# Differential attention in 1024-key score tiles: a two-layer encoder trunk on one core

## The chip, the core and the metric

The kernel runs on one NeuronCore of a Trainium2 chip. TensorE (PE; its weight loads are listed apart as PEld) multiplies matrices into PSUM, VectorE (DVE) and ScalarE (ACT) read PSUM and SBUF, GpSimd (POOL) works on SBUF alone, and SyncE (SP) issues the transfers. Each engine takes its instructions in the order in which they stand and waits at semaphores for the others. The metric is the device time of one execution in microseconds. For each kernel several executions are timed; one more is recorded by the profiler.

## The reference, cut to what matters

Two layers run over 2048 tokens of width 1024. Layer 0 (two kinds of banded attention) and the projections of layer 1 stay as they are. What changes is layer 1's differential attention: eight heads, each with two score maps whose softmaxes are subtracted before the product with the values, for rows of 128 queries over all keys up to the end of their own 64-token chunk.

```
s1 = q1 @ k1.T * scale;  s2 = q2 @ k2.T * scale        # 128 queries x all keys so far
p1 = softmax(where(mask, s1, NEG_INF));  p2 = softmax(where(mask, s2, NEG_INF))
o  = (p1 - lam * p2) @ v
o  = rms_norm(o, subln_g) * (1.0 - lambda_init)
y  = (o * silu(gate)) @ w_out;  x = x + y
```

Row t (0 to 15) sees 128(t+1) keys, so a head has 128 x 136 = 17,408 key columns in each of its two maps.

## The kernel before, in words

Every float32 operand of a product is split into a high and a low part (names ending in H and L), and a product is made of two or three matmuls. Layer 1 first projects (names that begin with p1) and then mixes: this is `_mix1`, whose tiles have names that begin with c.

`scores(h, b, K, res)` treats a block of four rows of head h. For each row and each of the two maps (m) it cuts the keys into pieces of at most 512. A piece gets a PSUM tile of one bank (tag S, four buffers), two matmuls (L842, L843), a VectorE maximum with the sign turned (L846), from the second piece on a running minimum with the piece before (L848), and on ScalarE the exponential with that maximum as its bias and with its sum collected (L850, which shows as ACTIVATE and as a READ_ACCUMULATOR). The last piece's masked corner is overwritten first (L845). So pieces of one row have different biases. A row with several pieces gets factors e from the biases (L855), and a VectorE instruction weighs and adds the sums (L856); GpSimd copies the first map's sum into a column (L858). VectorE then makes the reciprocal (L862), the factor of the last piece (L863) and those of the others (L865). The two maps are put together piece by piece: GpSimd scales the first map's earlier pieces by e (L869) and the second map's by its factor (L874), and adds (L875); every fifth piece is scaled and added by VectorE in one instruction instead (L872, `COMB`). Pieces of the first map live in a pool of 28 tiles of 512 columns (`pp`, tag P0), those of the second in six (tag P1).

`values(h, b, V, res)` takes the finished rows of a block: per 128 keys it transposes the pieces of four rows on TensorE into one bank (L889), splits the result with ScalarE (L892) and VectorE (L893), and adds three matmuls of up to 512 columns into a PSUM tile (L897 to L899). The output goes through ScalarE (L904) to memory.

A third stream, `gates()`, makes the gate projection with dense matmuls (L198 to L200, tile cG). `pace` interleaves the three as they are written down: scores run ahead of values by at most `LAG1` units (a unit is 256 score columns or one transposed 128 x 128 piece), gates by their share. From this program order a scheduler sets the order on each engine; gate matmuls may not stand ahead of the score matmul noted in `self.anchor`. At the end of `pace`, and in the `weave` after it, come the norm and the gate product (`finish`, with two P1 tiles per head, L1006 and L1008) and the output projection (`out_tile`, whose PSUM tiles have the tag S and whose residual tiles have the tag P1). The pool `pp` also holds the weights of layer 1's projection, and at the end output weights.

Of the kernel before, what the change touches and what calls it, by code (L numbers as in the profile page):

```python
# [18 lines left out]
P = 128  # L19
S = 2048  # L20
# [48 lines left out]
class Trunk:  # L69
# [4 lines left out]
    COMB = 5  # L74
    LAST = (0, 3, 2, 1)
    BANKS1, LAG1, SHARE1 = (4, 2, 1, 1), 65, 1.0
# [131 lines left out]
    def _project(self, es, layer):  # L208
# [21 lines left out]
        def weight_tiles():  # L230

            i = chunks[0] % 12 if layer == 0 else None
            chunks[0] += 1
            for part in "HL":
                if layer == 1:
                    yield self.pp.tile([P, 512], F32R, tag="P0", name=n + "w" + part)
# [547 lines left out]
    def layer1(self, steps=("project", "mix")):  # L784
        pool = self.tc.tile_pool
        with pool(name="hv", bufs=2) as self.hv, pool(name="pp", bufs=28, side="right") as self.pp:
            if "project" in steps:
                self.project(1)
            if "mix" in steps:
                self.mix1()  # L790
# [5 lines left out]
    def _mix1(self, es):  # L796
# [19 lines left out]
        count = [0]  # L816

        def scores(h, b, K, res):
# [3 lines left out]
            for m in range(2):  # L822
                r = slice(m * HD, (m + 1) * HD)
                for part, q in (("qH", qd), ("qL", ql)):
                    nc.sync.dma_start(f32(q[0:HD, m, :]), s[part][h, r, tok])
                    nc.sync.dma_start(f32(q[HD:P, m, :]), s[part][h, r, tok])
            us = res["u"] = []
            l1 = small("l1", NTB)
            for j in range(NTB):
                t = b * NTB + j  # L830
                nk = (t + 1) * P
                cuts = [(c, min(nk, c + 512)) for c in range(0, nk, 512)]
                nb = len(cuts)
                js = slice(j * P, (j + 1) * P)
                pr = []
                for m in range(2):
                    nm, la, chunks = small("nm", 4), small("la", 4), []
                    for z, (c, ce) in enumerate(cuts):
                        wd = ce - c
                        ps = pS.tile([P, 512], F32, tag="S", name=n + "S")[:, :wd]  # L840
                        kt = K[z][m]
                        mm(ps, qd[:, m, js], kt[:, :wd], start=True, stop=False)  # L842
                        self.anchor = mm(ps, ql[:, m, js], kt[:, :wd], start=False, stop=True).ins  # L843
# [3 lines left out]
                        if z:  # L847
                            nc.vector.tensor_tensor(nm[:, z:z + 1], nm[:, z:z + 1], nm[:, z - 1:z], ALU.min)  # L848
                        chunks.append((sb if m else pp).tile([P, 512], F32, tag=f"P{m}", name=n + f"P{m}", bufs=6 if m else 28))
                        nc.scalar.activation(chunks[z][:, :wd], ps, AF.Exp, bias=nm[:, z:z + 1], accum_out=la[:, z:z + 1])  # L850
                        yield wd / 256
                    l, e = la[:, 0:1], None
                    if nb > 1:
                        e, l, pe = small("e", 4), small("l"), small("pe", 4)
# [264 lines left out]
```

## Time and profile before

| | us |
|---|---|
| three timed executions | 2973.82, 2973.92, 2978.35 (median 2973.92) |
| profiled execution, its own time | 2979.35 |
| its span, first to last instruction | 2977.6 |
| first and last score matmul of layer 1 (L843) begin | 1827.0 and 2698.8 |
| mean granted TensorE clock | 0.966 |

Rows of a profile name the line of the kernel, the engine, the operation, the tile written and the tiles read with their buffer numbers left out, the shapes (partitions x elements), the count, the busy time and the mean of one. In the views that have it, idle time of the engine just ahead of the instruction follows, and behind an arrow whoever released it. Rows of the windows give the start and end of a stretch, its length, and busy time per engine. Matmuls overlap: one's listed duration is longer than the distance to the next one's start.

### The profile page before, as it was taken

The numbers are of one execution on the slowest core, as the hardware profiler recorded it, in microseconds if no ns is written. First come the engines' busy times: TensorE is split into PE (matmuls) and PEld (weight loads), VectorE is DVE, ScalarE is ACT, GpSimd is POOL, SyncE is SP. The second block draws the span as 40 slices with busy tenths as digits, with TensorE's granted clock in tenths as the row PEclk, the third lists the DMA queues.
The fourth block names the chain that finished last, engine by engine and source line by source line (L and its number), as shares of the span: only waits on it lengthen the run. The fifth ranks groups of instructions, "written<-read, shape, count | busy, mean of one in ns | idle before, by whom it ended". The sixth has DMA issues, their size and how long they took to land. (4 is left out here: it accounts for less than half of the span.)

```text
span 2977.6 us, 45362 instructions
## 1 busy us (share of the span) xinstructions
PE 2738.9 (92%) x13672; PEld 2253.3 (76%) x13672; DVE 2113.1 (71%) x5516; ACT 1615.0 (54%) x4167; POOL 1537.2 (52%) x1774
## 2 busy tenths in 40 slices
PE   7999999997888889899999999899999999986898
PEld 5888888876777778777788887677777777864776
DVE  7652475156767775589638844999998999986673
ACT  4443543266656665343343323677776777765552
POOL 3542252145334343357645732776766777775552
PEclk9999999999999999999999999999999999997999
DMA  4673344569988885657884456356546546425443
GB/s 156 224 249 121 103 149 128 186 190 258 256 218 219 221 216 146 213 207 239 268 290 155 129 182 200 111 141 188 166 121 187 161 133 194 141 80 153 138 131 104
DMA packets 349973, 526.28 MB, mean 177 GB/s; under 512 B 42272, under 2 KB 143648, under 8 KB 349728
## 3 DMA queue, kind: packets, MB, share of 16 engines
q1 hardware_dynamic: 349728, 523.38, 59.7%
q8 instruction: 109, 1.79, 0.3%
q14 instruction: 136, 1.11, 0.1%
HBM read 354.42 MB, written 168.82 MB: 176 GB/s over the span
## 5 line engine op out<-in xcount | busy, mean ns | idle before, releaser
L850 ACT ACTIVATE cP<-cS,cnm 128x512 f32<-128x512 f32 (+3 forms) x640 | 399.4, 628 | 191.3 <-DVE cnm L848 111.9
L846 DVE TENSOR_REDUCE cnm<-cS 128x1 f32<-128x512 f32 (+3 forms) x640 | 374.7, 598 | 26.3 <-PE cS L843 21.8
L198 PE MATMUL p1mm<-p1wH,p1hH 128*128 128x512 f32 x768 | 304.7, 397 | 0.0
L199 PE MATMUL p1mm<-p1wL,p1hH 128*128 128x512 f32 x768 | 304.4, 396 | 0.0
L200 PE MATMUL p1mm<-p1wH,p1hL 128*128 128x512 f32 x768 | 302.9, 395 | 0.0
L842 PE MATMUL cS<-ck,cqd 128*128 128x512 f32 (+3 forms) x640 | 265.7, 417 | 36.7 <-ACT cP L850 29.2
L286 POOL TENSOR_TENSOR p0wL<-p0ws,p0wH 128x512 fp32r<-128x512 f32 (+1 forms) x128 | 155.5, 1248 | 276.7 <-ACT p0wH L285 263.7
L875 POOL TENSOR_TENSOR cP<-cP,cP 128x512 f32<-128x512 f32 (+3 forms) x256 | 284.5, 1126 | 3.3
L874 POOL TENSOR_SCALAR cP<-cP,ccs 128x512 f32<-128x512 f32 (+3 forms) x256 | 176.4, 698 | 170.3 <-DVE ccs L863 67.2
L198 PE MATMUL p0mm<-p0wH,p0hH 128*128 128x512 f32 (+1 forms) x640 | 237.6, 374 | 3.9 <-ACT p0vt L436 3.1
L843 PE MATMUL cS<-ck,cql 128*128 128x512 f32 (+3 forms) x640 | 237.5, 373 | 1.8 <-DMA cql<-qL 1.8
L199 PE MATMUL p0mm<-p0wL,p0hH 128*128 128x512 f32 (+1 forms) x640 | 237.7, 372 | 0.0
L200 PE MATMUL p0mm<-p0wH,p0hL 128*128 128x512 f32 (+1 forms) x640 | 237.5, 372 | 0.2 <-DVE p0hL L311 0.2
L286 POOL TENSOR_TENSOR p1wL<-p1ws,p1wH 128x512 fp32r<-128x512 f32 x128 | 167.8, 1333 | 95.3 <-ACT p1wH L285 80.7
L893 DVE TENSOR_TENSOR cptL<-ctr,cptH 128x512 fp32r<-128x512 f32 (+1 forms) x320 | 190.3, 597 | 17.9 <-ACT cptH L892 17.1
L842 PEld LDWEIGHTS cS<-ck,cqd 128*128 128x128 f32 x640 | 124.2, 194 | 82.9 <-ACT cP L850 67.6
L892 ACT ACTIVATE cptH<-ctr 128x512 fp32r<-128x512 f32 (+1 forms) x320 | 168.5, 535 | 33.2 <-PE ctr L889 32.6
L889 PE MATMUL ctr<-ident,cP 128*128 128x128 f32 x1088 | 181.5, 282 | 1.1 <-POOL cP L875 0.9
L198 PEld LDWEIGHTS p1mm<-p1wH,p1hH 128*128 128x128 f32 x768 | 145.1, 189 | 30.4
L200 PEld LDWEIGHTS p1mm<-p1wH,p1hL 128*128 128x128 f32 x768 | 145.0, 189 | 30.3 <-issue 0.2
L199 PEld LDWEIGHTS p1mm<-p1wL,p1hH 128*128 128x128 f32 x768 | 145.0, 189 | 29.2
L889 PEld LDWEIGHTS ctr<-ident,cP 128*128 128x128 f32 x1088 | 139.1, 145 | 36.0 <-issue 4.0
(311 smaller groups left out, 8011.1 us busy)
## 6 DMA issues: line engine op xcount, KB each, us to landing
p1ws<-in_od_w_in_dram SPq DMA_DIRECT2D x56, 512.0 KB, 4.4
p0ws<-in_ev_w_in_dram SPq DMA_DIRECT2D x48, 512.0 KB, 4.4
cqd<-qH SPq DMA_DIRECT2D x128, 128.0 KB, 4.4
cql<-qL SPq DMA_DIRECT2D x128, 128.0 KB, 4.3
cwH<-wgH SPq DMA_DIRECT2D x32, 512.0 KB, 4.6
cwL<-wgL SPq DMA_DIRECT2D x32, 512.0 KB, 5.8
mvB<-bv SPq DMA_DIRECT2D x24, 512.0 KB, 6.9
mvA<-av SPq DMA_DIRECT2D x24, 480.0 KB, 5.4
```

Source lines behind the costliest of these rows:

```text
L198: mm(ps, aH, bH, start=first, stop=False)
L199: mm(ps, aH, bL, start=False, stop=False)
L200: mm(ps, aL, bH, start=False, stop=last)
L286: nc.gpsimd.tensor_tensor(l[:, :width], ws[:, k, :width], f32(h[:, :width]), ALU.subtract)
L842: mm(ps, qd[:, m, js], kt[:, :wd], start=True, stop=False)
L843: self.anchor = mm(ps, ql[:, m, js], kt[:, :wd], start=False, stop=True).ins
L846: nc.vector.tensor_reduce(nm[:, z:z + 1], ps, AX.X, ALU.max, negate=True)
L850: nc.scalar.activation(chunks[z][:, :wd], ps, AF.Exp, bias=nm[:, z:z + 1], accum_out=la[:, z:z + 1])
L874: nc.gpsimd.tensor_scalar(p2, p2, cc, 1.0, ALU.mult, ALU.mult)
L875: nc.gpsimd.tensor_tensor(p1, p1, p2, ALU.add)
L889: nc.tensor.transpose(tp[:, (j - j0) * P:(j - j0 + 1) * P], us[j][kt // 4][:, kk:kk + P], self.ident)
L893: nc.vector.tensor_tensor(L[:, :wd], tp[:, :wd], f32(H[:, :wd]), ALU.subtract)
```

## The change

Score tiles take up to 1024 keys: tag S has two buffers of two banks each, where it had four of one bank (`BANKS1`). A tile gets two or four matmuls, one maximum and one exponential. A row has at most two pieces, so that the running minimum, the factor e and the sums occur once per map, in rows 8 to 15 alone. The weighted sum of the two collected sums, the last piece's factor and the other piece's factor are now one-column instructions on GpSimd (new L881, L886, L888); the copy of the sum is gone. The second map is always scaled on GpSimd (new L891); the earlier piece, 1024 wide, is scaled and added to it by VectorE (new L893), the last piece is added on GpSimd (new L895). `COMB` is gone.

Rows 0 to 3 and 4 to 7 stay groups of four; rows 8 to 15 are values groups of two rows, whose transposes put two times 128 keys of two rows in one bank and whose matmuls have 256 columns. Queries are still loaded per block of four (`queries`). The pool `pp` is cut into 8 tiles of 1024 (PA) and 12 of 512 (PB), P1 into 3 of 1024; the uses of the pool outside the attention follow. `LAG1` goes from 65 to 48.

```diff
-    COMB = 5
+    WIDE, NARROW = 8, 12
-    BANKS1, LAG1, SHARE1 = (4, 2, 1, 1), 65, 1.0
+    BANKS1, LAG1, SHARE1 = (2, 2, 1, 1), 48, 1.0
...
+        groups = [(4 * b + i, 4 * b + i + n) for b in range(NB) for n in ((4,) if b < 2 else (2,)) for i in range(0, 4, n)]
...
-                cuts = [(c, min(nk, c + 512)) for c in range(0, nk, 512)]
+                cuts = [(c, min(nk, c + 1024)) for c in range(0, nk, 1024)]
...
-                        ps = pS.tile([P, 512], F32, tag="S", name=n + "S")[:, :wd]
-                        kt = K[z][m]
-                        mm(ps, qd[:, m, js], kt[:, :wd], start=True, stop=False)
-                        self.anchor = mm(ps, ql[:, m, js], kt[:, :wd], start=False, stop=True).ins
+                        ps = pS.tile([P, 1024], F32, tag="S", name=n + "S")[:, :wd]
+                        for k in range(c, ce, 512):
+                            w = min(ce - k, 512)
+                            kt, o = K[k // 512][m], ps[:, k - c:k - c + w]
+                            mm(o, qd[:, m, js], kt[:, :w], start=True, stop=False)
+                            self.anchor = mm(o, ql[:, m, js], kt[:, :w], start=False, stop=True).ins
+                            if k + w < ce:
+                                yield w / 256
...
-                            nc.vector.tensor_tensor(nm[:, z:z + 1], nm[:, z:z + 1], nm[:, z - 1:z], ALU.min)
+                            nc.vector.tensor_scalar(nm[:, 1:2], nm[:, 1:2], nm[:, 0:1], None, ALU.min)
...
-                        nc.vector.tensor_tensor_reduce(pe[:, :nb], e[:, :nb], la[:, :nb], 1.0, 0.0, ALU.mult, ALU.add, l)
-                    if m == 0:
-                        nc.gpsimd.tensor_scalar(l1[:, j:j + 1], l, 1.0, 1.0, ALU.mult, ALU.mult)
+                        nc.gpsimd.tensor_scalar(l, la[:, 0:1], e, la[:, 1:2], ALU.mult, ALU.add)
...
-                nc.vector.scalar_tensor_tensor(cs[:, nb - 1:nb], la1, self.nlam, rl, ALU.mult, ALU.mult)
+                nc.gpsimd.tensor_scalar(cs[:, nb - 1:nb], rl, la1, self.nlam, ALU.mult, ALU.mult)
                 if nb > 1:
-                    nc.vector.tensor_scalar(cs[:, :nb - 1], e2[:, :nb - 1], cs[:, nb - 1:nb], None, ALU.mult)
+                    nc.gpsimd.tensor_scalar(cs[:, 0:1], e2, cs[:, 1:2], 1.0, ALU.mult, ALU.mult)
                 for z, (c, ce) in enumerate(cuts):
+                    nc.gpsimd.tensor_scalar(p2, p2, cs[:, z:z + 1], 1.0, ALU.mult, ALU.mult)
                     if z < nb - 1:
-                        nc.gpsimd.tensor_scalar(p1, p1, e1[:, z:z + 1], 1.0, ALU.mult, ALU.mult)
-                    count[0] += 1
-                    if count[0] % self.COMB == 0:
-                        nc.vector.scalar_tensor_tensor(p1, p2, cc, p1, ALU.mult, ALU.add)
+                        nc.vector.scalar_tensor_tensor(p1, p1, e1, p2, ALU.mult, ALU.add)
                     else:
-                        nc.gpsimd.tensor_scalar(p2, p2, cc, 1.0, ALU.mult, ALU.mult)
                         nc.gpsimd.tensor_tensor(p1, p1, p2, ALU.add)
...
+            each = NTB // (r1 - r0)
+            for k0 in range(0, r1, each):
...
+                for kt, i0, c, wd in parts:
+                    o, lastk = O[:, i0 * P:], kt == r1 - 1
+                    mm(o, vH, H[:, c:c + wd], start=(kt == 0), stop=False, skip_group_check=True)
+                    mm(o, vH, L[:, c:c + wd], start=False, stop=False, skip_group_check=True)
+                    mm(o, vL, H[:, c:c + wd], start=False, stop=lastk, skip_group_check=True)
```

TensorE, the second map of a row 8, before: three pieces, each with its own PSUM tile. ck is a tile of 512 keys, cG the gate product, cO the values' output.

```order
L842 MATMUL cS<-ck_24072,cqd 128x512
L843 MATMUL cS<-ck_24072,cql 128x512
L198 MATMUL cG<-cwh,cwH 128x512
L199 MATMUL cG<-cwh,cwH 128x512
L200 MATMUL cG<-cwh,cwL 128x512
L842 MATMUL cS<-ck_24247,cqd 128x512
L843 MATMUL cS<-ck_24247,cql 128x512
L897 MATMUL cO<-cptH,cwv 128x512
L842 MATMUL cS<-ck_24605,cqd 128x128
L843 MATMUL cS<-ck_24605,cql 128x128
L898 MATMUL cO<-cptL,cwv 128x512
L899 MATMUL cO<-cptH,cwv 128x512
```

The same place now: the first four score matmuls fill one tile of two banks, with a gate product between its halves, and the next two fill the other tile.

```order
L863 MATMUL cS<-ck_23606,cqd 128x512
L864 MATMUL cS<-ck_23606,cql 128x512
L198 MATMUL cG<-cwh,cwH 128x512
L199 MATMUL cG<-cwh,cwH 128x512
L200 MATMUL cG<-cwh,cwL 128x512
L863 MATMUL cS<-ck_23799,cqd 128x512
L864 MATMUL cS<-ck_23799,cql 128x512
...
L863 MATMUL cS<-ck_24045,cqd 128x128
L864 MATMUL cS<-ck_24045,cql 128x128
L915 MATMUL ctr<-ident,cPA 128x128 x2
L863 MATMUL cS<-ck_23603,cqd 128x512
```

The last row begins row 9's first map, in the buffer of the wide tile; between the two stand the gate product that is left out here, the 128-wide tile and two transposes.

VectorE around the end of a row 8, before. cnm holds the maxima, cptL a low part of transposed pieces, cpe and cl the weighted sums (L856 is listed as two rows), ccs the factors.

```order
L848 TENSOR_TENSOR cnm_23028<-cnm_23028 128x1
L846 TENSOR_REDUCE cnm_23083<-cS_23085 128x1
L893 TENSOR_TENSOR cptL_23100<-ctr_23094,cptH_23099 128x512
L846 TENSOR_REDUCE cnm_23083<-cS_23106 128x1
L856 ISA cpe_23068,cl_23067<-ce_23066,cla_23029 128x3
L856 ISA cl_23067 128x1
L848 TENSOR_TENSOR cnm_23083<-cnm_23083 128x1
L862 RECIPROCAL crl_23071<-cl_23067 128x1
L863 SCALAR_TENSOR_TENSOR ccs_23072<-cl_23023,nlam_110,crl_23071 128x1
L865 TENSOR_SCALAR ccs_23072<-ce_23066,ccs_23072 128x2
L872 SCALAR_TENSOR_TENSOR cP0_23020<-cP1_23064,ccs_23072,cP0_23020 128x128
```

VectorE at the same place now. The reciprocal takes cl from GpSimd, and the wide instruction takes cP1 from GpSimd.

```order
L869 TENSOR_REDUCE cnm_22747<-cS_22749 128x1
L885 RECIPROCAL crl_22738<-cl_22736 128x1
L868 MEMSET cS_22781 64x64
L869 TENSOR_REDUCE cnm_22747<-cS_22781 128x1
L920 TENSOR_TENSOR cptL_22912<-ctr_22906,cptH_22911 128x512
L871 TENSOR_SCALAR cnm_22747<-cnm_22747 128x1
L920 TENSOR_TENSOR cptL_22940<-ctr_22934,cptH_22939 128x512
L893 SCALAR_TENSOR_TENSOR cPA_22668<-cPA_22668,ce_22678,cP1_22707 128x1024
```

Three small instructions left the queue, and two of those that stay wait for GpSimd with reduces of the next row behind them.

126 lines of the change are left out of this document (77 added, 49 removed).

## The prediction

> **What bounds the kernel now.** I read the busy time by stage first, the waits of the stage that the change touches next, then the groups of instructions there, and last a few microseconds of the time line for the distance of one start from the next. The page gives a span of 2977.6 us to a profiled execution of 2979.35 us; the sum below is made against that execution, which lies 5.4 us above the median of 2973.92, and the difference that it gives is taken from the median. The windows cut layer 1's mixing into its start, its main part, its last scores and the tail.
>
> ```profile
> core 0: us, PE busy (x) PEld busy (x) DVE busy (x) ACT busy (x) POOL busy (x), PEclk, DMA share, GB/s
> 1826.00:1926.00 100.00, 86.33 (x405) 65.81 (x405) 91.11 (x283) 70.44 (x212) 66.45 (x93) 0.95 0.36 106
> 1926.00:2626.00 700.00, 661.83 (x3365) 531.16 (x3366) 656.83 (x1978) 512.83 (x1513) 496.89 (x683) 0.98 0.54 157
> 2626.00:2712.00 86.00, 59.66 (x249) 42.35 (x249) 71.10 (x181) 57.36 (x149) 61.22 (x70) 0.84 0.40 116
> 2712.00:2978.00 266.00, 230.74 (x917) 178.99 (x915) 153.39 (x217) 120.77 (x211) 114.47 (x85) 0.90 0.43 126
> ```
>
> In the main part VectorE is busy for 656.8 of 700 us, 94%, and TensorE for about as much. The two do not mean the same: a matmul's listed time runs on under the next one's start. The tile of the scores gives the length of the loop, 1827.0 to 2698.8, or 871.8 us; the time lines of TensorE give the true pace.
>
> ```profile
> L843 PEld LDWEIGHTS cS<-ck,cql x640: 186/189/338, 1827.0 to 2698.4; 128*128 128x128 f32 x160
> L843 PE MATMUL cS<-ck,cql x640: 223/390/767, 1827.0 to 2698.8; 128*128 128x512 f32 x136, 128*128 128x128 f32 x8, 128*128 128x384 f32 x8, 128*128 128x256 f32 x8
> ```
>
> ```profile
> 2204.58 0.39 PE L843 MATMUL cS<-ck,cql 128*128 128x512 f32 x1
> 2204.82 0.39 PE L842 MATMUL cS<-ck,cqd 128*128 128x512 f32 x1
> ...
> 2207.94 0.60 PE L889 MATMUL ctr<-ident,cP 128*128 128x128 f32 x4
> 2208.29 0.48 PE L897 MATMUL cO<-cptH,cwv 128*128 128x512 f32 x1
> ```
>
> A matmul of 512 columns, listed with 0.39 us, is followed by the next 0.23 to 0.24 us later; four transposes take 0.35. At 0.23 per 512 columns the loop's matmuls (557,056 score columns, 393,216 of the gates, 391,680 of the values and 4,096 others, as the order has them up to the last score) come to 604.7 us, and its 1,028 transposes to 90.0: 694.7 us of dense work in 871.8. TensorE loses 177 us, a fifth, and the waits say to whom:
>
> ```profile
> ACT cP L850 <- DVE cnm L848: 111.9, 138, 4.0
> PEld cS L842 <- ACT cP L850: 67.6, 118, 2.6
> ...
> PEld cO L898 <- DVE cptL L893: 36.7, 45, 3.5
> PE cS L842 <- ACT cP L850: 29.2, 54, 2.2
> ```
>
> TensorE waits for a score buffer that ScalarE has yet to empty (67.6 and 29.2), ScalarE for a maximum from VectorE, 0.81 us each time (111.9 over 138). VectorE sets the pace; beside it TensorE waits for cptL and other work of the values, some 70 us in all.
>
> **The change part by part.** VectorE first, by the groups of this stage.
>
> ```profile
> L846 DVE TENSOR_REDUCE cnm<-cS 128x1 f32<-128x512 f32 (+3 forms) x640 | 374.7, 598 | 26.3 <-PE cS L843 21.8 <-DMA vH<-p1vH 2.1
> L893 DVE TENSOR_TENSOR cptL<-ctr,cptH 128x512 fp32r<-128x512 f32 (+1 forms) x305 | 181.9, 598 | 6.1 <-ACT cptH L892 5.3
> L848 DVE TENSOR_TENSOR cnm<-cnm 128x1 f32<-128x1 f32 x384 | 131.0, 343 | 1.5
> L856 DVE CUSTOM_DVE_ANT_0 cpe<-ce,cla 128x3 f32<-128x3 f32 (+2 forms) x191 | 59.1, 311 | 9.4 <-ACT ce L855 7.6 <-ACT cP L850 1.1
> L872 DVE SCALAR_TENSOR_TENSOR cP<-cP,ccs,cP 128x512 f32<-128x512 f32 (+2 forms) x63 | 50.7, 804 | 0.9
> L845 DVE MEMSET cS<- 64x64 f32 x256 | 28.4, 112 | 13.7 <-PE cS L843 11.1
> L863 DVE SCALAR_TENSOR_TENSOR ccs<-cl,nlam,crl 128x1 f32<-128x1 f32 x95 | 26.5, 279 | 0.9
> L865 DVE TENSOR_SCALAR ccs<-ce,ccs 128x1 f32<-128x1 f32 (+2 forms) x95 | 24.7, 260 | 0.6
> ```
>
> ```profile
> L846 DVE TENSOR_REDUCE cnm<-cS 128x1 f32<-128x512 f32 x448 | 300.7, 677 | 23.0 <-PE cS L843 21.8
> ...
> L846 DVE TENSOR_REDUCE cnm<-cS 128x1 f32<-128x128 f32 x64 | 17.9, 282 | 2.6 <-DMA vH<-p1vH 2.1
> ```
>
> A reduce has a fixed part of 0.150 us and 1.03 ns per key (677 less 282 ns over 384 keys). The keys stay; 640 reduces become 384, so 256 fixed parts go: 38 us. The running minimum falls from 384 to 128 (256 x 0.343 = 88), L856, L863 and L865 leave for GpSimd (59, 26 and 25), L872's 51 us go, and 64 wide instructions come that the trace does not show: 1.2 us each if priced like a reduce of 1,024 keys, 1.6 if priced as two of L872 at its mean of 0.804; I take the latter, the same operation, and 102 us. That is 185 us less of listed time. Listed times overlap (these eight rows alone add to 877 us, where the first three windows hold 819 of busy time), so I count 0.85 of it: 157 us less, 662 left, 77% of the loop that comes out below. VectorE stops being the bound.
>
> ```profile
> L875 POOL TENSOR_TENSOR cP<-cP,cP 128x512 f32<-128x512 f32 x173 | 221.5, 1293 | 0.9
> L874 POOL TENSOR_SCALAR cP<-cP,ccs 128x512 f32<-128x512 f32 x173 | 134.0, 785 | 64.2 <-DVE ccs L865 22.8 <-DVE ccs L863 21.2 <-ACT cP L850 6.1
> ...
> L858 POOL TENSOR_SCALAR cl<-cl 128x1 f32<-128x1 f32 x96 | 20.2, 211 | 3.4 <-DVE cl L856 1.8 <-DVE crl L862 0.7 <-DVE cnm L848 0.3
> ```
>
> GpSimd now scales all 139,264 columns of the second map (at 785 ns per 512, at most 214 us), adds only 73,728 (at 1,293 per 512, at most 186) and gets 320 one-column instructions (0.211 each, 68): at most 468 us, where it had 625 in these windows. That is hidden under 860 us of TensorE, as long as nobody waits for a single result. ScalarE loses 256 fixed parts of its exponentials and as many reads of the sum:
>
> ```profile
> L850 ACT ACTIVATE cP<-cS,cnm 128x512 f32<-128x512 f32 x448 | 309.1, 693 | 151.0 <-DVE cnm L848 88.2 <-DVE cnm L846 53.6 <-DVE cl L856 5.9
> ...
> L850 ACT ACTIVATE cP<-cS,cnm 128x128 f32<-128x128 f32 x64 | 23.8, 373 | 13.6 <-DVE cnm L848 9.1 <-DVE cnm L846 3.8 <-DVE el L877 0.5
> ```
>
> The exponential costs 0.267 us and 0.833 ns per key, so at least 68 of its 641 us go, and ScalarE was not the bound before. The matmuls keep their columns; narrower value groups only make 1,200 of them 256 wide, against 96 before, and those cost half of a full one:
>
> ```profile
> 2203.08 0.28 PE L899 MATMUL cO<-cptH,cwv 128*128 128x256 f32 x1
> 2203.20 0.23 PE L897 MATMUL cO<-cptH,cwv 128*128 128x128 f32 x1
> ```
>
> 0.12 us from start to start, with the next weights loaded underneath. The Trainium skill speaks against this step: its page "TensorE: Matmul & The Clock Gate", section "Back-to-back issue gap", gives about 81 ns per matmul of 128 columns and 131 of 512 in a stream of weight loads and matmuls, so a narrow one costs more per column; an estimate half way between, 0.75 of a full one, would add some 63 us here. The trace does not agree: 0.12 against 0.23. Through `LAG1` some 4 us of value work (7,296 columns and 11 transposes) move from behind the last score to ahead of it: the loop's dense work is 698.8 us, and the tail has 4 us less.
>
> What is late next is the score buffer. Before, four tiles were in flight, now two, and a wide one is freed late:
>
> ```profile
> 2205.01 0.69 DVE L846 TENSOR_REDUCE cnm<-cS 128x1 f32<-128x512 f32 x1 [0.27 <-PE cS L843]
> ...
> 2206.05 0.71 ACT L850 ACTIVATE cP<-cS,cnm 128x512 f32<-128x512 f32 x1
> ...
> 2206.90 0.50 PE L842 MATMUL cS<-ck,cqd 128*128 128x512 f32 x1 [0.17 <-ACT cP L850]
> ```
>
> A reduce that waits for nothing else starts 0.43 us after its last matmul (2204.58), 0.20 after TensorE goes on; TensorE starts 0.14 after the exponential that frees its buffer (2206.76). For 1,024 keys: 0.20 + 1.20 + 1.12 + 0.14, and 0.04 for the step to ScalarE, makes 2.7 us, if VectorE and ScalarE are free at once. In that time TensorE must find other work. In the quoted place at row 8 it has, from the end of the wide tile to the next wide one, a gate product, the 128-wide tile and two transposes, 0.99 us, and so 1.7 us are lost. Counted over the order, 78 of the 160 wide tiles have less than 2.7 us between, 0.9 us short on the mean; in the order before, with four buffers and a chain of 1.75, 9 of 444 full pieces. Going once down TensorE's order at these prices, and holding each score tile until the one before last is free, TensorE loses 84 us if nobody queues, 128 if each tile also meets a queue of 0.4 us, and 180 at 0.8; 0.1 us of queue costs about 12 us.
>
> The queue is the unknown. Below it is bounded by 0, above by the 0.81 us that ScalarE waited per time under a VectorE that was 94% busy. I take 0.4: VectorE's other work, some 345 us of 860, stands ahead of a ready tile four times in ten with about half of 0.7 us, ScalarE's (a quarter of its time) with half of 0.55, which makes 0.21, and twice that because both queues keep an order fixed beforehand. Of the 80 us that TensorE lost otherwise (177 less 97) I leave 35, as VectorE's load falls. Loop: 698.8 + 128 + 35 = 862 us against 871.8, 10 less; with the 4 of the tail 14 less. The tail keeps its streams; P1's three tiles there are covered by the 35 of 266 us in which TensorE is idle, and cost up to 1 us for each of 32 output tiles if that cover is gone. 2973.9 less 14 is **2960 us**.
>
> **The rivals.** *The queue hardly counts:* ring at 84, other losses 15, loop 798, 78 us less, 2896 us. For it speaks that every engine but TensorE falls below 80%; against it that the order has wide tiles almost side by side. *One for one:* with a queue of 0.46 to 0.56 us the new ring costs what VectorE cost, and the time moves by less than 6 us, 0.2%, about what a measurement of this kernel can tell from no change. *VectorE held by GpSimd, slower:* before, no large VectorE instruction waited for GpSimd; now the reciprocal and the wide instruction do, 64 times each, with the next row's reduces queued behind them in the order. GpSimd's chain for a row (two sums, two factors, and two scales of up to 1.6 us each at L874's price) has to end in time; if a reduce is held for 0.4 us more on the mean, the queue is 0.8, the ring 180 and the loop 914: 38 us more, 3012 us. It decides from a queue of 0.56 on. *Weight loads:* if each matmul of 256 columns takes the 0.19 of a weight load instead of 0.12, 1,104 more of them cost 77 us and make 3037; the 0.12 above speaks against it. The page's rule named there points the same way, with 63 us by its figures. *The tail:* P1's cover gone, 32 us, 2992.
>
> **How the numbers follow.** Forecast (6 to 40 us less, 2934 to 2968) 0.40; the queue hardly counts 0.14; one for one 0.14; VectorE held 0.27; weight loads 0.03; tail 0.02. Faster 0.54, within 0.2% 0.14, slower 0.32. The range runs from 2900, nearly no queue, to 3010, a queue of nearly 0.8; outside lie parts of three cases, under 2 in 10.
>
> **What would show it.** Right: VectorE at 75 to 80% in the loop, the reduce at 1.2 us and the exponential at 1.1 for 1,024 keys, GpSimd under 470 us, and TensorE's waits for a score buffer at 100 us or more with ScalarE as releaser, ahead of the first matmul of wide tiles. Wrong: waits of the reciprocal or the wide instruction for GpSimd of 30 us and more (held), waits for buffers under 60 us (no queue), 256-wide matmuls 0.17 or more apart, or a tail longer than 275 us.

## The result, and the profile after

| | us |
|---|---|
| before, median of 4 (2973.82 to 2981.37) | 2976.14 |
| after, median of 4 (3092.55 to 3111.40) | 3107.38 |
| ratio, 95% interval | 1.0429 (1.039 to 1.0468) |
| profiled execution after, its span | 3110.43, 3108.7 |

The change is slower by 131 us; forecast were 14 us less, in a range that ended at 3010. In the lines of the changed kernel the score matmuls are L863 and L864, the maximum L869, its minimum L871, the exponential L874, the wide VectorE instruction L893, the transposes L915 and their split L919 and L920. The same stages as before, in the windows of the changed kernel, and last its whole loop:

```profile
core 0: us, PE busy (x) PEld busy (x) DVE busy (x) ACT busy (x) POOL busy (x), PEclk, DMA share, GB/s
1855.00:1955.00 100.00, 85.03 (x426) 69.26 (x427) 73.07 (x140) 57.24 (x134) 47.00 (x67) 0.91 0.38 112
1955.00:2748.00 793.00, 692.40 (x3842) 578.12 (x3841) 585.23 (x1066) 455.55 (x1046) 396.68 (x521) 0.95 0.49 141
2748.00:2834.00 86.00, 61.16 (x306) 49.77 (x304) 69.46 (x113) 52.86 (x112) 50.60 (x59) 0.87 0.34 92
2834.00:3108.00 274.00, 231.72 (x934) 183.37 (x933) 146.66 (x218) 124.71 (x215) 122.34 (x90) 0.89 0.42 126
...
1855.00:2834.00 979.00, 838.59 (x4570) 697.15 (x4570) 727.76 (x1318) 565.65 (x1289) 494.29 (x646) 0.94 0.46 134
```

The tile of the scores gives the loop:

```profile
L864 PE MATMUL cS<-ck,cql x640: 272/393/632, 1855.2 to 2833.6; 128*128 128x512 f32 x136, 128*128 128x128 f32 x8, 128*128 128x384 f32 x8, 128*128 128x256 f32 x8
```

From 1855.2 to 2833.6 it takes 978.4 us, 107 more than 871.8. It begins 28 us later than before, and the tail is 4 us shorter (275.1). VectorE is busy for 728 of the loop's 979 us: the engine that set the pace has a quarter of its time free, and the loop is longer. The waits within the loop say where TensorE stands:

```profile
ACT cptH L919 <- PE ctr L915: 113.2, 103, 4.2
...
PEld cS L863 <- ACT cP L874: 47.4, 53, 2.7
PEld cS L863 <- ACT cPA L874: 40.7, 46, 2.3
...
PE cS L863 <- ACT cP L874: 33.3, 39, 2.4
...
PE cS L863 <- ACT cPA L874: 28.1, 30, 2.1
PEld cS L863 <- ACT cPB L874: 24.5, 22, 2.2
...
PEld ctr L915 <- DVE cPA L893: 21.6, 13, 3.0
...
PE cS L863 <- ACT cPB L874: 18.0, 17, 2.1
PE ctr L915 <- DVE cPA L893: 16.0, 13, 2.5
DVE cPA L893 <- POOL cP L891: 13.0, 17, 1.4
...
DVE crl L885 <- POOL cl L881: 10.8, 11, 1.7
```

One stall of TensorE shows in two rows, at the weight load and at the matmul behind it: all 86 waits of score matmuls for a buffer stand behind a weight load that waits for the same buffer (before, all 54). So the rows are not to be added. Waits for a score buffer are 113 us on the weight loads, where they were 68, and 79 on the matmuls, where they were 29; the stall lies between the two, since the first begins while an earlier matmul still runs and the second is short of a listed duration that is too long. New are some 20 us (21.6 and 16.0) in which transposes wait for the wide instruction; and ScalarE now waits 113 us for transposes (24.6 before): TensorE is late itself. The groups of VectorE and GpSimd, duration last:

```profile
L869 DVE TENSOR_REDUCE cnm<-cS 128x1 f32<-128x1024 f32 x159 | 193.7, 1219 | 56.5 <-PE cS L864 55.2
...
L893 DVE SCALAR_TENSOR_TENSOR cPA<-cPA,ce,cP 128x1024 f32<-128x1024 f32 x64 | 133.4, 2085 | 13.2 <-POOL cP L891 13.0
```

```profile
L891 POOL TENSOR_SCALAR cP<-cP,ccs 128x1024 f32<-128x1024 f32 x79 | 88.5, 1121 | 0.7
L881 POOL TENSOR_SCALAR cl<-cla,ce 128x1 f32<-128x1 f32 x128 | 75.9, 593 | 309.8 <-ACT ce L879 309.8
L886 POOL TENSOR_SCALAR ccs<-crl,cl,nlam 128x1 f32<-128x1 f32 x126 | 42.5, 338 | 203.6 <-DVE crl L885 134.7 <-DMA cwL<-wgL 61.2 <-DVE cS L868 7.6
```

One wide tile of row 14, in the time line, shows the whole chain:

```profile
2556.03 2.84 DVE L893 SCALAR_TENSOR_TENSOR cPA<-cPA,ce,cP 128x1024 f32<-128x1024 f32 x1 [0.90 <-POOL cP L891]
...
2557.67 0.63 PE L863 MATMUL cS<-ck,cqd 128*128 128x512 f32 x1
...
2557.78 1.30 POOL L881 TENSOR_SCALAR cl<-cla,ce 128x1 f32<-128x1 f32 x1
...
2558.09 0.63 PE L864 MATMUL cS<-ck,cql 128*128 128x512 f32 x1
...
2558.80 1.21 DVE L869 TENSOR_REDUCE cnm<-cS 128x1 f32<-128x1024 f32 x1
...
2560.69 1.09 ACT L919 ACTIVATE cptH<-ctr 128x512 fp32r<-128x512 f32 x2 [4.19 <-PE ctr L915]
...
2561.66 1.12 ACT L874 ACTIVATE cP<-cS,cnm 128x1024 f32<-128x1024 f32 x1
...
2562.92 0.19 PEld L863 LDWEIGHTS cS<-ck,cqd 128*128 128x128 f32 x1 [1.39 <-ACT cP L874]
2562.92 0.67 PE L863 MATMUL cS<-ck,cqd 128*128 128x512 f32 x1 [1.20 <-ACT cP L874]
```

The maximum stands 0.71 us behind its last matmul, for the wide instruction that ran 2.84 us; the exponential waits 1.65 us behind the maximum's end at 2560.01, since ScalarE's order has the copies L919 ahead of it, and they wait for TensorE. The last two rows are one stall. Over all 160 tiles of 1024 keys the trace gives these means: 0.99 us from the last matmul's start to the maximum (0.43 when nothing is ahead), 0.41 from its end to the exponential (0.03 at the least), and 3.74 from the last matmul's start to the end of the exponential. Without the two waits it would be 2.79, so that is a queue of 0.95 us. In the kernel before, the same measure over its 448 pieces of 512 keys gives 3.91 us, with a queue of 2.1.

### The profile page after: what moved, and what is told of

The parts are those of the page before. It is cut to its first block, busy times and chain, and to the rows that moved or that the text cites. A ratio compares the mean times of both kernels' runs of the same rounds, so it can differ in the third digit from the quotient of the medians.

```text
span 3108.7 us, 44486 instructions
## 1 busy us (share of the span) xinstructions
PE 2780.6 (89%) x14248; PEld 2322.7 (75%) x14248; DVE 2022.2 (65%) x4396; ACT 1544.4 (50%) x3591; POOL 1414.0 (45%) x1582
## 4 chain that ended last, share of the span: by engine, by line
PE 53%; DVE 16%; DMA 12%; ACT 5%; issue 4%; POOL 3%; SPq 1%; DVEq 0%; ACTq 0%; POOLq 0%
PE p1mm L200 4%; PE p1mm L198 4%; PE p1mm L199 4%; DVE cnm L869 3%; PE cS L863 3%; PE cS L864 3%; DVE cPA L893 3%; PE p0mm L198 2%; PE p0mm L199 2%; PE p0mm L200 2%; PE ctr L915 2%; PE cO L926 2%; PE mom L198 1%; PE mom L199 1%; DMA cog<-o 1%
## 5 line engine op out<-in xcount | busy, mean ns | idle before, releaser
L869 DVE TENSOR_REDUCE cnm<-cS 128x1 f32<-128x1024 f32 (+7 forms) x384 | 348.4, 909 | 62.4 <-PE cS L864 55.2
L863 PE MATMUL cS<-ck,cqd 128*128 128x512 f32 (+3 forms) x640 | 269.6, 422 | 89.4 <-ACT cP L874 33.3
L864 PE MATMUL cS<-ck,cql 128*128 128x512 f32 (+3 forms) x640 | 240.9, 382 | 3.7 <-DMA cql<-qL 3.7
L920 DVE TENSOR_TENSOR cptL<-ctr,cptH 128x512 fp32r<-128x512 f32 (+3 forms) x304 | 187.9, 627 | 68.9 <-ACT cptH L919 67.5
L863 PEld LDWEIGHTS cS<-ck,cqd 128*128 128x128 f32 x640 | 128.2, 200 | 137.3 <-ACT cP L874 47.4
L874 ACT ACTIVATE cP<-cS,cnm 128x1024 f32<-128x1024 f32 (+2 forms) x192 | 166.2, 866 | 118.9 <-DVE cnm L869 63.8
L919 ACT ACTIVATE cptH<-ctr 128x512 fp32r<-128x512 f32 (+3 forms) x304 | 163.7, 551 | 120.6 <-PE ctr L915 116.5
L881 POOL TENSOR_SCALAR cl<-cla,ce 128x1 f32<-128x1 f32 x128 | 75.9, 593 | 309.8 <-ACT ce L879 309.8
L926 PE MATMUL cO<-cptL,cwv 128*128 128x256 f32 (+3 forms) x512 | 162.4, 317 | 24.1 <-DVE cptL L920 23.8
L915 PE MATMUL ctr<-ident,cPA 128*128 128x128 f32 x928 | 161.0, 291 | 21.6 <-DVE cPA L893 16.0
L874 ACT ACTIVATE cPA<-cS,cnm 128x1024 f32<-128x1024 f32 (+3 forms) x128 | 132.3, 1034 | 84.5 <-DVE cnm L869 61.4
L891 POOL TENSOR_SCALAR cP<-cP,ccs 128x640 f32<-128x640 f32 (+4 forms) x192 | 170.5, 896 | 4.4
L925 PE MATMUL cO<-cptH,cwv 128*128 128x256 f32 (+3 forms) x512 | 160.5, 314 | 10.6 <-ACT cptH L919 8.7
L198 PE MATMUL p1mm<-p1w,p1hH 128*128 128x512 f32 x400 | 158.7, 398 | 0.0
L199 PE MATMUL p1mm<-p1w,p1hH 128*128 128x512 f32 x400 | 158.2, 395 | 0.6 <-POOL p1w L294 0.6
L200 PE MATMUL p1mm<-p1w,p1hL 128*128 128x512 f32 x400 | 158.6, 397 | 0.0
L927 PE MATMUL cO<-cptH,cwv 128*128 128x256 f32 (+3 forms) x512 | 154.2, 301 | 0.0
```

The costliest lines, as they stand in the source:

```text
L198: mm(ps, aH, bH, start=first, stop=False)
L199: mm(ps, aH, bL, start=False, stop=False)
L200: mm(ps, aL, bH, start=False, stop=last)
L863: mm(o, qd[:, m, js], kt[:, :w], start=True, stop=False)
L864: self.anchor = mm(o, ql[:, m, js], kt[:, :w], start=False, stop=True).ins
L869: nc.vector.tensor_reduce(nm[:, z:z + 1], ps, AX.X, ALU.max, negate=True)
```

## The experiments

Differences are between medians; the median of the kernel before itself lay between 2974.6 and 2981.0 from one experiment to the next, so under 8 us nothing is read from two of them.

**The ring.** e2_half_max shortens one part of the chain:

```diff
-nc.vector.tensor_reduce(nm[:, z:z + 1], ps, AX.X, ALU.max, negate=True)
+nc.vector.tensor_reduce(nm[:, z:z + 1], ps[:, :min(wd, 512)], AX.X, ALU.max, negate=True)
```

> The changed kernel with the maximum of a score tile taken over at most its first 512 columns, and with layer 1's queries scaled down so that nothing overflows; what is left out is the maximum over the other columns, some 110 us of VectorE (0.53 us for each of 160 tiles of 1024 keys, 0.13 to 0.40 for 96 others), all of it between the last matmul of a tile and the release of its buffer. Theory 'ring': TensorE waits for two buffers that are each held through filling, maximum and exponential; the chain gets 0.5 us shorter and the time falls by 50 to 70 us, to 3040 to 3055. Rival 'wide instruction': VectorE's 64 wide instructions of 2.09 us, in order ahead of maxima and transposes, hold things up; then this saves under 25 us, 3082 or more.

Measured: 3055.7 (ratio to before 1.0257, 1.0232 to 1.0283), 52 us less, as the ring has it: the mean of the 1024-key tiles is 3.23 us instead of 3.74, 0.51 less. VectorE is also busy for 97 us less in the loop, and e2 alone does not part the two.

e4_one_bank takes the tile apart:

```diff
-ps = pS.tile([P, 1024], F32, tag="S", name=n + "S")[:, :wd]      # two buffers
+o = pS.tile([P, 512], F32, tag="S", name=n + "S")[:, :w]         # four buffers, within the loop over k
```

> The changed kernel with score tiles of one bank in four buffers again: a maximum, a running minimum and an exponential for each 512 keys, as before; all else as changed (small products on GpSimd, the wide instruction, values of two rows, pools). The halves of a piece are not brought to one bias, so the output is another. VectorE gets some 92 us more (256 fixed parts of 0.15, 256 minima of 0.21). Theory 'ring': 60 to 110 us come back, 2995 to 3045, and TensorE's waits for a score buffer fall from 192 us listed to about 100. Rival 'wide instruction' or VectorE's load in general: with 92 us more on VectorE nothing comes back, 3100 to 3170.

Measured: 2991.3 (1.0043, 1.0021 to 1.0065): 116 us come back, though VectorE has more to do (757 us of the loop instead of 728). TensorE's waits for score buffers in the loop, which now lasts 872 us:

```profile
PEld cS L864 <- ACT cPA L873: 17.0, 28, 1.8
PEld cS L864 <- ACT cP L873: 13.7, 23, 2.6
...
PE cS L864 <- ACT cPA L873: 8.7, 13, 1.6
...
PE cS L864 <- ACT cP L873: 7.1, 9, 2.4
```

With 3.5 for cPB that is 34 us on the weight loads, where it was 113. The loop is 106 us shorter, 27 more than these waits: the rest is not time spent waiting for a buffer.

e6_two_bank_halves keeps e4's instructions and puts two pieces in one tile again:

```diff
+ps = pS.tile([P, 1024], F32, tag="S", name=n + "S")              # two buffers
-o = pS.tile([P, 512], F32, tag="S", name=n + "S")[:, :w]
+o = ps[:, k - c:k - c + w]
```

> The kernel with a maximum, a minimum and an exponential for each 512 keys (2991 us with four one-bank buffers), but with two such pieces in one tile of two banks and two such tiles, as in the changed kernel; the same instructions as in the run with one-bank tiles, only buffers are held longer; halves of a piece keep their own biases. Theory 'release': what costs is that two banks come free together, 3060 to 3110, nearly the changed kernel's 3107. Rival 'long instructions': what costs is the maximum of 1.22 and the exponential of 1.11 us one after the other; then halves that overlap filling, maximum and exponential stay near 2991, at most 3020.

Measured: 3366.6 (1.1304, 1.128 to 1.1327), 375 us more than with one-bank tiles and beyond both expectations. Its loop, in the windows and the waits:

```profile
1842.00:3110.00 1268.00, 979.40 (x4601) 750.92 (x4602) 821.32 (x1842) 659.50 (x1815) 473.33 (x653) 0.86 0.36 105
```

```profile
PEld cS L865 <- ACT cP L874: 134.8, 145, 2.6
...
PEld cS L865 <- ACT cPA L874: 120.7, 129, 3.3
```

The instructions are those of e4 and none is long. But the buffers' release is not all that changed. Here a row of 896 keys, its second map: the exponential of the first half, then the first matmul of the second half, which writes the other bank of the same tile.

```profile
2500.95 0.69 ACT L874 ACTIVATE cP<-cS,cnm 128x512 f32<-128x512 f32 x1
...
2501.78 0.44 PE L865 MATMUL cS<-ck,cqd 128*128 128x384 f32 x1 [0.20 <-ACT cP L874]
```

In all 48 tiles of rows 4 to 6, whose halves can be told apart by their width, the second half begins at the earliest 0.14 us after the end of the first half's exponential, in 15 of them just then. So e6 makes the halves of a tile go one after the other, which neither e4 nor the changed kernel does. How much of its 375 us is the price of that is not known, and so it does not separate the release of two banks together from the longer instructions. Both belong to how long a buffer is held, and which of them costs more stays open. That the ring of two two-bank buffers costs, e4 shows, and e2 agrees.

**The wide instruction.** e3_no_wide and e5_one_bank_no_wide leave it out, under two buffers and under four:

```diff
-if z < nb - 1:
-    nc.vector.scalar_tensor_tensor(p1, p1, e1, p2, ALU.mult, ALU.add)
-else:
+if z == nb - 1:
     nc.gpsimd.tensor_tensor(p1, p1, p2, ALU.add)
```

> The changed kernel without the wide VectorE instruction (L893); what is left out is the sum of the earlier pieces of both maps in rows 8 to 15, 133 us of VectorE, none of it between a matmul and the release of its buffer. Theory 'wide instruction': TensorE's transposes no longer wait for it (21.6 and 16.0 us), ScalarE's exponentials neither (19.9), no maximum stands behind it, and the time falls by 60 us or more, to 3047 or less. Rival 'ring': the chain of a tile stays but for a shorter queue; the time falls by 20 to 40 us, 3067 to 3087, less than with the shorter maximum although more VectorE time goes.

> The kernel with score tiles of one bank in four buffers (the run before, 2991 us), now also without the wide VectorE instruction; the sum of the earlier pieces in rows 8 to 15 is left out, and the halves of a piece keep their own biases. Under two buffers of two banks its removal was worth 73 us (3107 to 3034). Theory 'made dear by the ring': the instruction mostly delays maxima that two buffers cannot ride out, and with four buffers its removal is worth at most 35 us, 2956 or more. Rival 'dear by itself': it costs its place on VectorE and the transposes behind it whatever the ring, 60 to 75 us again, 2916 to 2931.

Measured: 3034.1 (1.0186, 1.017 to 1.0202), 73 us less; and 2928.8 (0.9835, 0.9801 to 0.987), 62 less than 2991.3. The instruction is dear by itself, with four buffers too; that the ring makes it dear is not borne out. In e3 the maximum of a wide tile starts 0.62 us after the last matmul instead of 0.99. Ring and instruction nearly add up: 116 and 73 make 189, taken off together they bring 179. Both runs leave out work that the kernel needs, and with it what that work costs anywhere.

e13_wide_unread lets it write over its other operand, and e11_split_wide cuts it in two:

```diff
-nc.vector.scalar_tensor_tensor(p1, p1, e1, p2, ALU.mult, ALU.add)
+nc.vector.scalar_tensor_tensor(p2, p1, e1, p2, ALU.mult, ALU.add)                                   # e13
+for x in (slice(0, 512), slice(512, 1024)):                                                         # e11
+    nc.vector.scalar_tensor_tensor(p1[:, x], p1[:, x], e1, p2[:, x], ALU.mult, ALU.add)
```

> The changed kernel with the wide VectorE instruction writing over its second-map operand instead of the first-map tile: the same work on VectorE, and its wait for GpSimd's scale stays, but no transpose waits for it; what is left out is its result in the product with the values. Without the instruction the time was 3034, with it 3107. Theory 'time on VectorE': nothing comes back, 3095 to 3115. Rival 'the transposes wait for it': most of the 73 us comes back, 3035 to 3070.

> The changed kernel with the wide VectorE instruction in two of 512 columns each. Before, an instruction of that kind over 512 columns took 0.876 us, the wide one takes 2.085. Nothing is left out. Theory 'long hold': two times 0.88 is 0.33 us less for each of 64, and a maximum can go between them: 15 to 35 us less, 3072 to 3092. Rival 'load': what counts is the time on VectorE, 21 us listed, of which at most half shows: under 12 us, 3095 or more.

Measured: 3088.0 (1.038, 1.0345 to 1.0414), 19 less: between the two, with the larger part, some 54 of 73 us, in its time on VectorE. And 3107.3 (1.0439, 1.0418 to 1.0459): no gain. The group of e11 says why the halves were not shorter:

```profile
L894 DVE SCALAR_TENSOR_TENSOR cPA<-cPA,ce,cP 128x512 f32<-128x512 f32 x128 | 141.4, 1144 | 11.9 <-POOL cP L891 11.7
```

Two times 1144 ns is 2288, more than 2085. What lengthens them is in the last section.

**The lead and the start.** e12_lag65 and e15_one_bank_lag65 set `LAG1` from 48 to 65 in the changed kernel and in e4_one_bank, e14_before_lag48 sets 48 in the kernel before.

> The changed kernel with LAG1 at 65, as before, instead of 48: scores run further ahead of values. Nothing is left out. Theory 'values too close behind': TensorE's transposes wait less for the wide instruction (21.6 and 16.0 us listed) and the time falls by 10 to 30 us, 3077 to 3097. Rival 'the ring decides': the waits for score buffers stay, and a longer tail or full pools take back what the transposes gain; 3097 to 3120.

> The kernel with one-bank score tiles in four buffers and the rest as changed (2991 us at LAG1 48), now at 65; the halves of a piece keep their own biases. Theory 'apart from the ring': 20 to 35 us less again, 2956 to 2971. Rival 'the lead matters only where the ring is tight': under 8 us, 2983 or more.

> The kernel before with LAG1 at 48 instead of 65. Nothing is left out. In the changed kernel 65 instead of 48 brought 31 us. Theory 'the lead counts by itself': 20 to 40 us more, 2996 to 3016. Rival 'it counts only with the changed kernel's long way from score to transpose': within 8 us, 2968 to 2984.

Measured: 3076.1 (1.0333, 1.0309 to 1.0356), 31 less; 2970.9 (0.999, 0.9977 to 1.0003), 20 less than 2991.3; 2984.4 (1.0025, 1.0 to 1.0051), some 10 more (0 to 15 by the interval), between the two expectations. So the lead counts with both rings, and seems to count more than in the kernel before; that the transposes now wait for the wide instruction is the likely reason, and was not tried by itself.

e1_gap puts an unused tile between two pools:

```diff
 sm = pool("sm", 8)
+pool("gap", 1).tile([P, 104], F32, tag="gap", name=n + "gap")
 ld = pool("ld", 2)
```

> The changed kernel with 416 unused bytes per partition between the pool of small tiles and the pool of the queries, so that the queries' tiles lie where they lay before. In the changed kernel the first query loads are issued at 1846.9 us, right after the last store of vL (1844.8), where before they were issued at 1765.7; TensorE stands still from 1843.0 to 1855.2 but for one matmul. Theory 'placed over': the smaller small tiles moved the query tiles over memory that the projection holds to its end. Then the loads go out some 60 us ahead of the first score matmul again, TensorE's gap closes, and the time falls by 8 to 14 us, to about 3096. Rival 'order of the queue': the loads come late because of the program order alone; then nothing moves (3107, within 6).

Measured: 3092.2 (1.0383, 1.0366 to 1.0399), 15 less. First the start in the changed kernel, then the first query load in e1_gap, both from time lines:

```profile
1844.80 0.32 SPq L458 DMA_DIRECT2D vL<-p1vL  x1
1846.95 0.45 SPq L834 DMA_DIRECT2D cqd<-qH  x1
...
1851.05 0.45 PE L863 MATMUL cS<-ck,cqd 128*128 128x128 f32 x1 [7.63 <-DMA cql<-qL]
...
1855.17 0.45 PE L864 MATMUL cS<-ck,cql 128*128 128x128 f32 x1 [3.68 <-DMA cql<-qL]
```

```profile
1770.62 0.45 SPq L835 DMA_DIRECT2D cqd<-qH  x1
```

Fewer small columns had moved the queries' tiles onto memory that the projection uses until its end. Of the 28 us by which the loop began later, 12 are this gap. Some 10 are the projection itself: from its first to its last matmul it takes 581 to 585 us in the seven kernels with separate weight tiles and 590 to 596 in the thirteen with joint ones; why was not tried. The other 6 were there before it began, in code that the change does not touch; that beginning lies between 1234 and 1260 us over all kernels.

**VectorE's and GpSimd's small work.** e7_before_min writes the minimum of the kernel before as the change has it, e9_before_factors moves its factors to GpSimd, e10_before_min_factors does both, e18_before_min_comb is e7 with `COMB` 10:

```diff
-nc.vector.tensor_tensor(nm[:, z:z + 1], nm[:, z:z + 1], nm[:, z - 1:z], ALU.min)
+nc.vector.tensor_scalar(nm[:, z:z + 1], nm[:, z:z + 1], nm[:, z - 1:z], None, ALU.min)              # e7
-nc.vector.scalar_tensor_tensor(cs[:, nb - 1:nb], la1, self.nlam, rl, ALU.mult, ALU.mult)
+nc.gpsimd.tensor_scalar(cs[:, nb - 1:nb], rl, la1, self.nlam, ALU.mult, ALU.mult)                   # e9, and L865 alike
```

> The kernel before with the running minimum (L848) written as the changed kernel has it, an instruction with a per-partition operand instead of one with two tensors: 384 times 0.210 us where it was 0.343, 51 us of listed VectorE time less and the chain of 384 pieces 0.13 us shorter. Nothing is left out. Theory 'VectorE sets the pace before' (94% busy): 20 to 45 us less, 2933 to 2958. Rival 'TensorE and the order set the pace': under 8 us, 2970 or more.

> The kernel before with the factors of a row (L863, L865) as one-column to three-column instructions on GpSimd, as the changed kernel has them; the weighted sum L856 stays on VectorE. Nothing is left out. VectorE has 65 us less to do (26.5, 14.0 and 24.7 listed), GpSimd some 70 us more of 872. Theory 'VectorE sets the pace before' (taking 51 us off it brought 37): 25 to 50 us less, 2925 to 2950. Rival 'the hand-over to GpSimd and its 0.3 us eat it': under 8 us, 2968 or more.

> The kernel before with the running minimum by a per-partition operand (alone: 2938 us) and the factors on GpSimd, both; nothing is left out; 116 us less on VectorE, with the ring of four one-bank buffers. Theory 'VectorE sets the pace': another 20 to 40 us, 2898 to 2918. Rival 'once is enough': VectorE was already below 93% and the rest is TensorE's order and GpSimd at over 80%; 2925 to 2945.

> The kernel before with the cheaper running minimum (2938 us) and with every tenth piece instead of every fifth scaled and added on VectorE (COMB 10), the others on GpSimd; nothing is left out; some 25 us more off VectorE, some 60 more on GpSimd (now 611 of 833). Theory 'VectorE still sets the pace': 8 to 18 us less, 2920 to 2930. Rival 'no longer': within 6 us or slower, 2932 to 2950, as the factors on GpSimd brought nothing either.

Measured: 2937.9 (0.9868, 0.9844 to 0.9891); 2970.2 (0.9976, 0.9958 to 0.9993), some 9 less; 2937.8 (0.9875, 0.985 to 0.9899); 2937.5 (0.9855, 0.9831 to 0.9878). The minimum alone brings 38 us, and nothing on top of it brings more. In e10 VectorE is busy for 740 us of the loop, 32 less than in e7, and GpSimd for 674, 62 more; in e18 VectorE has only 6 us less. So VectorE's load may no longer bound the loop, or the work that GpSimd got takes the gain back: this is not separated. e7, e10 and e18 are alike, and the fastest of the kernels here that compute all of the reference. The tile of the minimum, first before, then in e7 (shortest, median, longest):

```profile
L848 DVE TENSOR_TENSOR cnm<-cnm x384: 132/158/1332, 1840.7 to 2702.3; 128x1 f32<-128x1 f32 x192
```

```profile
L848 DVE TENSOR_SCALAR cnm<-cnm x384: 136/202/218, 1838.2 to 2665.2; 128x1 f32<-128x1 f32 x192
```

The median is longer; what goes is a tail of up to 1.33 us. The last section comes back to it.

e8_before_pairs gives the kernel before the values groups of two rows, e16_small_on_vector moves L881, L886 and L888 of the changed kernel from `nc.gpsimd` to `nc.vector`, and e17_three_undone puts e1, e12 and e16 together.

> The kernel before with values groups of two rows from row 8 on and nothing else (matmuls 256 wide, transposes of two rows and two key tiles in a bank, the output of two rows at a time; LAG1 stays 65). Nothing is left out. My prediction priced this part at nothing: 2968 to 2986. Rival 'narrow groups cost': more steps that wait for cptL, and 1,104 more matmuls of 256 columns; 15 us or more, 2993 or higher.

> The changed kernel with the weighted sum of the two sums and both factors of a row (L881, L886, L888) on VectorE instead of GpSimd, in the same form. Nothing is left out. Theory 'VectorE held by GpSimd', the slower rival of my prediction: the reciprocal and the wide instruction no longer wait for GpSimd's 0.59 and 0.34 us instructions, 20 us or more less, 3087 or below. Rival 'not held': 320 instructions of 0.2 to 0.35 us, 60 to 110 us more on VectorE, and nothing gained: 3105 to 3160.

> The changed kernel with three parts undone together: queries back in their place (alone 15 us), LAG1 at 65 (31), the small products on VectorE (23); nothing is left out, and the two two-bank buffers, the wide instruction and the narrow groups stay. Theory 'they add': 69 us less, 3033 to 3045, and some 60 us are the ring's and the wide instruction's. Rival 'they share one wait': the latter two cover the same stalls, 3050 to 3075.

Measured: 2974.5 (0.9994, 0.9981 to 1.0007), no cost; 3084.3 (1.037, 1.0353 to 1.0388), 23 less, as my slower rival has it; 3077.7 (1.0329, 1.03 to 1.0358), 29 less and not 69. The three do not add, and the gain is smaller than either expectation allowed: e17 is no faster than e12 alone, whose loop lasts 942 us against 959. With the gap alone the loop is as long as without (981 and 978), so at a lead of 65 the small products on VectorE seem to cost; e16's gain is then no price of the hand-over to GpSimd that adds to the others. About 100 of the 131 us remain with the ring, the wide instruction and the longer projection (some 10).

## Why the prediction was wrong

**The step that failed** is the term for the other losses: "Of the 80 us that TensorE lost otherwise (177 less 97) I leave 35, as VectorE's load falls". The 97 adds the waits of the weight loads (67.6) to those of the matmuls behind them (29.2), which are the same stalls. Taken once, TensorE lost 68 us to buffers and 109 otherwise, and the 109 did not fall with VectorE's load. The table gives what the runs show: the loop, the waits for a score buffer on the weight loads, and the rest of the loop beyond these and the dense work (698.8 us, or 694.7 at a lead of 65).

| kernel | loop | waits for a buffer | other losses |
|---|---|---|---|
| forecast | 862 | 128 | 35 |
| before | 871.8 | 68 | 109 |
| changed | 978.4 | 113 | 167 |
| e3, no wide instruction | 904.2 | 84 | 121 |
| e4, four one-bank buffers | 872.4 | 34 | 139 |
| e5, both at once | 802.4 | 20 | 84 |
| e12, lead 65 | 942.3 | 113 | 134 |

VectorE's share fell from 94 to 74%, and the other losses grew by 58 us instead of falling by 74. The wide instruction accounts for 46 of the 167 (e3), the lead for 33 (e12), the ring for 28 (e4); these shares overlap. Within them are the transposes that wait for the wide instruction, and a granted clock of 0.94 in the loop instead of 0.96: by an estimate 16 us (698.8 / 0.94 less 698.8 / 0.96). A step moved by `LAG1` was priced by its matmuls, not by who then waits.

**The queue** came out otherwise too: "The queue is the unknown. Below it is bounded by 0, above by the 0.81 us that ScalarE waited per time under a VectorE that was 94% busy. I take 0.4". It measured 0.95, beyond the bound. A tile passes two queues in turn, 0.56 us at VectorE and 0.38 at ScalarE, and one wait of ScalarE could not bound both; the trace before had 2.1 by the same measure. But the price per queue was too high: 12 us for 0.1 makes some 195 us of waits at 0.95, and 113 are listed. So it is luck that the ring's term of 128 came near. In e2, 0.51 us less of chain took 29 us from these waits and 52 from the time, where the slope gives 61.

The freed VectorE halved the queue, but the longer instructions took it back: a buffer of 512 keys was held for 0.30 us of filling, 3.91 of chain and 0.14 of restart, four in flight; one of 1024 is held for 1.19, 3.74 and 0.14, two in flight. That is an estimate of 471 columns per us that the ring can pass before and 404 now. It gives the direction, not the size: e4 comes to 503 by the same count, and its loop is no shorter than that of the kernel before.

**The wide instruction**: 1.6 us each by L872's mean, measured 2.085, and its absence is worth 62 to 73 us. It was counted as load alone. With four buffers the kernel takes 2929 us without it and 2991 with it, where the kernel before takes 2976.

**The start** (15 us by e1) was in no term: the sum began at the first score matmul, and loads were not followed on SyncE's queue.

**Right** were the maximum (1.20, measured 1.219) and the exponential of 1024 keys (1.12, measured 1.11), VectorE's share nearly (77%, measured 74%), the waits for buffers as the sign to look for, and the narrow groups: e8 shows no cost, and the time line of the changed kernel has its matmuls of 256 columns 0.11 to 0.12 us apart:

```profile
2400.11 0.28 PE L927 MATMUL cO<-cptH,cwv 128*128 128x256 f32 x1
2400.22 0.28 PE L925 MATMUL cO<-cptH,cwv 128*128 128x256 f32 x1
2400.34 0.28 PE L926 MATMUL cO<-cptL,cwv 128*128 128x256 f32 x1
```

The tail is 4 us shorter, as forecast, but that is no more than luck: over all kernels here it lies between 258 and 286 us. GpSimd's one-column instructions took 135 us, not 68, and GpSimd 494, not 468. In the sentence on narrow matmuls, half way between the two figures is 0.81 of a full one (79 us) and not 0.75 (63); the sum did not use it. **The slower rival** had the sign right and the place only in part: VectorE's waits for GpSimd (13.0, 10.8 and 3.9 us) stay under its own mark of 30.

What stays open is how the lead, the small products, the wide instruction and the ring share the other losses: only sums of them were measured.

## What to carry to other kernels

Count a stall once: it shows in the waits of a weight load and again in those of the matmul behind it. Before a loss is priced as falling, say who causes it; here the other losses grew while VectorE's load fell. Fewer, larger PSUM tiles in the same banks keep the same bytes in flight but hold each longer; before merging two buffers into one, compare the holding time (filling, each queue, each instruction), not the engines' busy time. A chain through two engines in order meets both their queues. Where VectorE sets the pace beside a busy GpSimd, look first at its instructions with two SBUF operands, however small.

## What the runs showed of the hardware

**VectorE and GpSimd shut each other out.** Of the 64 wide instructions the two beside which GpSimd worked for less than a fifth of their time took 1.20 and 1.27 us; the 35 with GpSimd busy nearly throughout took 2.24 on the mean, 3.38 at most. The one-column L881 took 0.337 us in the 88 cases that no wide instruction overlaps and 1.157 in the 40 that one does. The minimum of two tensors (L848, before) took 0.149 us in 118 cases without GpSimd and 0.429 in 266 beside it; the form with one tensor is 0.20 in both. The maximum, which reads PSUM, keeps to its 1.22. The Trainium skill, page "SBUF — State Buffer", section "Who interferes with whom", says that a VectorE operation with two SBUF inputs contends with a GpSimd operation that reads SBUF, that contention for the ports they share is an exclusive lock, and that a reduce never contends; these numbers agree. They also fit blocks as long as the other engine's instruction: 512 columns on VectorE took 0.87 us before, beside GpSimd instructions of 0.79 and 1.29, and 1.14 in e11, beside such of 1.12 and 2.40. If so, two times L872 was too little for the wide instruction.

**TensorE's clock is lower where the stalls are more.** The granted clock in the loop is 0.94 in the changed kernel, 0.96 in the one before, 0.86 in e6 (above), and in e5, whose loop is the shortest:

```profile
1843.00:2650.00 807.00, 766.36 (x4576) 665.16 (x4576) 648.19 (x1770) 626.65 (x1805) 458.58 (x650) 0.98 0.57 164
```

The order is not strict: e12's loop of 942 us has 0.96 too. Where the clock is down, TensorE's work takes longer: the matmuls of the chain quoted first start 0.42 us apart (2557.67 and 2558.09) instead of 0.23, and the granted clock from 2557 to 2559 is 0.50. So a stall can cost more than its length. The Trainium skill, page "TensorE: Matmul & The Clock Gate", section "A second HAM failure mode: psum-queue depth-cycling", describes TensorE idling briefly on its PSUM buffers and the clock going up and down with it; the runs agree in kind.
